# A long-convolution block: magnitudes summed before their products, two of five inverse tables used whole in f32, and a reordered start

## The chip, the cores and the metric

The kernel is one program on one core of a Trainium2 chip. The metric is the device time of one execution in microseconds (us); lower is better. Times stand as the median of a few runs. The profile is of one further execution.

## The reference, cut to what matters

The whole model is two blocks on 512 positions (528 with 16 meta positions), width 1024. The change touches the first layer alone, a gated long convolution over 2048 channels:

```
u = rmsnorm(h) @ w_in + b_in                       # 528 x 8192
x0, x1, v = split(short_conv(u[:, :6144])); z = u[:, 6144:]
h_fwd, h_bwd = filters(w1..w4) * decay / (sum |filters| + 1e-6)
taps = concat(h_fwd, 0, h_bwd[:0:-1])
y  = irfft(rfft(v * x1, 2T) * rfft(taps, 2T))[:T] + skip * (v * x1)
h += rmsnorm((y * x0 * silu(z)) @ w_out)
```

The transforms are products with cosine and sine tables. `sum |filters|` runs over positions and both directions and gives one number per channel. After this layer come a differential-attention layer and a second block (sparse attention and a mixture of experts); the change leaves both as they are.

## The kernel before, in words

TensorE does the work in one of two forms. A *split* operand is a pair of fp32r tiles, high part and low part; a product of two split operands is three fp32r products (high-high, high-low, low-high). A *whole* operand is a plain f32 tile, and its product is one call. A split costs ScalarE one cast (L328, or L282 for weights) and VectorE or GpSimd one subtraction (L329, or L263 for weights).

Python loops are unrolled. The framework orders each engine's instructions itself, by a simulated timeline; `issue_after(x)` queues the instructions of a block behind x on x's engine, and `high_priority` moves work forward. Every engine then runs its queue strictly in that order. A tile name has `bufs` slots; a new tile of the name waits until the slot's last reader is done.

**Start** (`small_vectors` L513, `load_x` L544). SP's queue loads x, then the small vectors `sva`, `svb`, `svc` (L516 to L526), then the weights `wraw` (L232). ScalarE squares and sums x in five pieces (L563), each into a slot of `hTd` (2 slots). x is transposed into PSUM tile `ps` (2 slots, L582), copied to `hTd` (L584), stored to DRAM (L588), scaled by gain and norm (`xnf`, L593) and split into `xh`, `xl`. The gains come from `vc`, the transposed `svc`. The first product of the layer needs `xh`, `xl`, a split weight, and a free slot of `ps`. The split of the first weight job is queued behind the scaling `normed` on VectorE, that of the second behind the copy `copied` (third pair of columns) on ScalarE.

**Spectra** (`filter_spectra` L701, interleaved with the first half of the input projection `hyena_in`, up to about 345 us). For each of 8 quarters q of 256 channels it forms even and odd filters for three tiles of positions (128, 128 and 9 rows), takes magnitudes `mg` on ScalarE (L741) and their maximum on VectorE (L745); GpSimd adds the two directions (L747). TensorE then sums over positions by products with a column of ones (L790): 2 halves of channels x 3 tiles of positions a quarter, whole f32, reduced on VectorE (L791). The spectra go to DRAM (`Hdram`).

**Convolution** (`hyena_conv` L852, about 545 to 720 us). The inverse tables `gm` come by GpSimd's queue (L864). For each of 8 quarters: `fold` makes even and odd parts, transposes and splits them; five frequency tiles m = 0 to 4 are formed by split products (`ph`, L188), multiplied by the spectrum `hsp` (loaded by ScalarE's queue, L954) on VectorE (L960 to L962) and combined on GpSimd into `o` (L964, L966). `o` is split for m < 4 into `oh`, `ol`; m = 4 (17 rows, kept in 64-row tiles `orem`, shown as `or`) is split by four 17-row instructions (L975, L976). `inverse` runs one quarter behind: for each of 2 channel tiles and 2 sides it accumulates 15 products into `ps` (3 for each m), and ScalarE, VectorE and GpSimd form y (L902 to L909), which is split at the end of the quarter. Behind the last quarter comes the output projection (`pj`, L811 to L815).

Of the kernel before, what the change touches and what calls it, by code (L numbers as in the profile page):

```python
# [10 lines left out]
FT = mybir.dt.float32  # L11
FR = mybir.dt.float32r
# [3 lines left out]
OP = mybir.AluOpType  # L16
# [26 lines left out]
def host_consts():  # L43
# [83 lines left out]
    G[4, 32:32 + 9, 1, :n] = ge_im[256:265]  # L127
    gh, gl = _hi_lo(G)
    c["idft"] = np.ascontiguousarray(np.stack([gh, gl], axis=2).transpose(0, 1, 2, 3, 4))

    inv = (F32(10000.0) ** (-np.arange(0, 64, 2, dtype=F32) / F32(64))).astype(F32)
# [194 lines left out]
def split(k, raw, hi, lo, lo_eng=None):  # L326
    nc = k.nc
    nc.scalar.copy(hi, raw)  # L328
    (lo_eng or nc.vector).tensor_tensor(lo, raw, hi.bitcast(FT), OP.subtract)  # L329

# [178 lines left out]
def small_vectors(k, A, pp):  # L509
# [4 lines left out]
    with tc.tile_pool(name="sv", bufs=1, reuse_waits="tile") as sp:  # L514
        a = sp.tile([128, 128], FT, name="sva")
        nc.sync.dma_start(a[0:64], A["hy_b_in"][0].rearrange("(r c) -> r c", c=128))  # L516
        nc.sync.dma_start(a[64:112], A["hy_conv_b"][0].rearrange("(r c) -> r c", c=128))
        nc.sync.dma_start(a[112:128], A["hy_skip"][0].rearrange("(r c) -> r c", c=128))
        b = sp.tile([128, 128], FT, name="svb")
        c = sp.tile([64, 128], FT, name="svc")  # L520
        cw = A["hy_conv_w"][0].rearrange("t (r c) -> (t r) c", c=128)
        nc.sync.dma_start(b, cw[0:128])
        nc.sync.dma_start(c[0:16], cw[128:144])
        for i, (n, l) in enumerate((("norm_pre", 0), ("norm_pre", 1), ("norm_post", 0), ("norm_post", 1),
                                    ("norm_mix_2", 0), ("norm_ffn_2", 0))):
            nc.sync.dma_start(c[16 + 8 * i:24 + 8 * i], A[n][l].rearrange("(r c) -> r c", c=128))  # L526
# [18 lines left out]
def load_x(k, A, sp, pp):  # L545
# [15 lines left out]
    for i, (t0, n) in enumerate(TT):  # L561
        scr = sp.tile([128, 2, T], FT, name="hTd", bufs=2).rearrange("p a b -> p (a b)")[:, 0:D]
        nc.scalar.activation(scr[:n], xt[:n, i], AF.Square, accum_out=ss[:n, i:i + 1])  # L563
    rs = sp.tile([128, 5], FT, name="rs")
# [13 lines left out]
    for d0 in range(0, KD, 2):  # L578
        p = pp.tile([128, 2, 512], FT, name="ps", bufs=2)
        for j in range(2):  # L580
            for i in range(4):
                nc.tensor.transpose(p[:, j, i * 128:(i + 1) * 128], xt[:, i, (d0 + j) * 128:(d0 + j + 1) * 128], k.ident)  # L582
        hT = sp.tile([128, 2, T], FT, name="hTd", bufs=2)
        copied = nc.scalar.copy(hT[:, :, 0:512], p)  # L584
# [6 lines left out]
        for j in range(2):  # L591
            xn = sp.tile([128, T], FT, name="xnf", bufs=2)
            normed = nc.vector.scalar_tensor_tensor(xn, hT[:, j], k.gain(0, d0 + j), rbs, op0=OP.mult, op1=OP.mult)  # L593
            split(k, xn, k.xh[:, d0 + j], k.xl[:, d0 + j], nc.gpsimd if j else None)
        if d0 == 0:
# [29 lines left out]
def first_projection(k, A, C, pp):  # L625

    nc, tc = k.nc, k.tc
    with ExitStack() as ctx:
# [17 lines left out]
        for i in range(3):  # L646
# [52 lines left out]
def filter_spectra(k, A, C, hs, sp, wk, pp):  # L699
# [11 lines left out]
    for q in range(E // Q):  # L711
# [10 lines left out]
        mag = {}  # L722
        msum = []
        for s, op in ((0, OP.add), (1, OP.subtract)):
# [7 lines left out]
            for kt, (t0, n) in enumerate(KT):  # L732
# [53 lines left out]
            nc.sync.dma_start(k.Hdram[q4, 9:17, 9 - s, co], hsr[0:8, 1])  # L786
        p = pp.tile([128, 512], FT, name="pab", bufs=2)[:, 0:8].rearrange("p (c k) -> p c k", c=2)
        for c in range(Q // 128):
            for kt, (t0, n) in enumerate(KT):
                nc.tensor.matmul(p[:, c, kt:kt + 1], msum[kt][:n, c * 128:(c + 1) * 128], k.ones[:n], start=True, stop=True)  # L790
        nc.vector.tensor_reduce(tot[:, 2 * q:2 * q + 2], p[:, :, 0:3], AX.X, OP.add)  # L791
    nc.vector.tensor_scalar(tot, tot, 1e-6, None, op0=OP.add)
# [60 lines left out]
def hyena_conv(k, A, C, pp):  # L853
# [3 lines left out]
    with ExitStack() as ctx:  # L857
# [3 lines left out]
        sp = ctx.enter_context(tc.tile_pool(name="hc", bufs=1, reuse_waits="tile"))  # L861
        gm = sp.tile([128, 5, 2, 2, 266], FR, name="gm")
# [10 lines left out]
        for i in range(2):  # L873
            for s in range(2):
                vrem[i, s] = k.fold.tile([128, Q], FR, name=f"vr{i}{s}", bufs=1)
                nc.vector.memset(vrem[i, s].bitcast(FT), 0.0)
                orem[i, s] = sp.tile([64, Q], FR, name=f"or{i}{s}")
                nc.vector.memset(orem[i, s].bitcast(FT), 0.0)
        his, los = [], []

        def inverse(q, oh, ol):
            yy = wk.tile([128, NC, T], FT, name="y", bufs=1)
            for c in range(NC):
# [4 lines left out]
                for s in range(2):  # L888
                    p = pi[:, s, 0:266]
                    parts = []  # L890
                    for m in range(5):
                        sel = (0 if m < 2 else 1) if s == 0 else (1 if m < 2 else 0)
                        if m == 4:
                            a, b, n = oh[m][:, fs], ol[m][:, fs], 64
                        else:
                            a, b, n = oh[m][:, sel, fs], ol[m][:, sel, fs], 128
                        g0, g1 = gm[0:n, m, 0, s], gm[0:n, m, 1, s]
                        parts += [(a, g0), (a, g1), (b, g0)]
                    mmacc(nc, p, parts)
# [42 lines left out]
        for q in range(NQ):  # L942
# [6 lines left out]
            for m in range(5):  # L949
# [12 lines left out]
                nc.vector.tensor_tensor(t2[:n, 1], p[:n, 1], hsp[:n, 0], OP.mult)  # L962
                o = fw.tile([128, 2, Q], FT, name="o")
                nc.gpsimd.tensor_tensor(o[:n, 0], t1[:n, 0], t1[:n, 1], OP.subtract)  # L964
                d = slice(32, 32 + n) if m == 4 else slice(0, n)
                nc.gpsimd.tensor_tensor(o[d, 1], t2[:n, 0], t2[:n, 1], OP.add)  # L966
                if m < 4:
                    oh[m] = wk.tile([128, 2, Q], FR, name=f"oh{m}")
                    ol[m] = wk.tile([128, 2, Q], FR, name=f"ol{m}")
                    split(k, o, oh[m], ol[m])  # L970
                else:
                    oh[m], ol[m] = orem[q % 2, 0], orem[q % 2, 1]
# [1303 lines left out]
```

## Time and profile before

| | |
|---|---|
| runs, median (lowest to highest) | 2360.93 us (2360.74 to 2366.43), 3 runs |
| profiled execution, its own time | 2362.28 us |
| its span | 2360.5 us |
| PE busy | 2219.6 us, 94% of the span, 14332 instructions |
| DVE (VectorE) busy | 1537.9 us, 65% |
| ACT (ScalarE) busy | 1070.5 us, 45% |
| POOL (GpSimd) busy | 706.2 us, 30% |
| DMA | 306.18 MB, mean 130 GB/s |

PE is TensorE's products, PEld its weight loads, SP the engine that only issues DMAs. Products are pipelined, so the busy time of PE says little where starts are close together: the distance from one start to the next is what a product costs. PEclk is the granted share of TensorE's clock, 1.00 for 2.4 GHz and 0.50 for 1.2 GHz. In square brackets stands how long an engine was idle before an instruction and what it waited for. Names are out<-in, numbers of slots left out; a row with xN merges N instructions in succession. Times of rows are us from the span's start.

### The profile page before, as it was taken

To read this page: it belongs to the slowest core of one execution; us is meant where nothing else is said; L and a number is where in the kernel's file an instruction comes from. 1 tells how busy PE (TensorE), PEld (TensorE's weight loads), DVE (VectorE), ACT (ScalarE), POOL (GpSimd) and SP (SyncE) were. 2 spreads that over 40 slices of the span, in tenths; PEclk is the share of its full clock that TensorE was granted. 3 is DMA by queue.
4 is the path that set the end of the run, shared out by engine and by line. 5 is a ranking of instruction groups with operands and counts; after the bars stand their busy time and mean duration, and the time that the engine had idled before them with its cause. 6 is when DMAs were issued, how large, how long until landed. Compare 5 with 4: busy or idle time off the path is not lost. (4 is left out here: it accounts for less than half of the span.)

```text
span 2360.5 us, 37091 instructions
## 1 busy us (share of the span) xinstructions
PE 2219.6 (94%) x14332; PEld 1832.0 (78%) x14332; DVE 1537.9 (65%) x2852; ACT 1070.5 (45%) x2173; POOL 706.2 (30%) x705
## 2 busy tenths in 40 slices
PE   7999999998999989999999998989999999799997
PEld 6899989998889988898888887977666666534443
DVE  7688774546985578777868854568768655434434
ACT  5566653432334456655656644534444443222221
POOL 4455451114651333332323324623111103100100
PEclk9999999999999989999999998989899999899999
DMA  6433332232217522111211124652221235599991
GB/s 224 131 100 117 95 101 90 90 90 92 57 52 222 155 82 72 54 41 50 72 54 54 58 69 144 176 151 55 67 81 59 72 107 211 186 368 424 421 370 74
DMA packets 242060, 306.18 MB, mean 130 GB/s; under 512 B 20648, under 2 KB 208436, under 8 KB 233306
## 3 DMA queue, kind: packets, MB, share of 16 engines
q1 hardware_dynamic: 203328, 245.90, 30.8%
q10 hardware_dynamic: 33002, 32.64, 4.6%
q0 software_dynamic: 5552, 25.25, 2.9%
q8 instruction: 113, 1.85, 0.3%
q14 instruction: 65, 0.53, 0.1%
HBM read 278.19 MB, written 25.58 MB: 129 GB/s over the span
## 5 line engine op out<-in xcount | busy, mean ns | idle before, releaser
L263 DVE TENSOR_TENSOR wlo<-wraw,whi 128x1024 fp32r<-128x1024 f32 (+2 forms) x201 | 225.6, 1135 | 150.6 <-ACT whi L282 142.6
L263 POOL TENSOR_TENSOR wlo<-wraw,whi 128x1024 fp32r<-128x1024 f32 (+1 forms) x91 | 181.2, 1999 | 475.0 <-ACT whi L282 345.5
L282 ACT CAST whi<-wraw 128x1024 fp32r<-128x1024 f32 x198 | 205.9, 1047 | 171.4 <-PE ps L813 50.3
L811 PE MATMUL ps<-xh,whi 128*128 128x264 f32 x1024 | 214.3, 286 | 5.4 <-ACT hTd L584 5.1
L813 PE MATMUL ps<-xl,whi 128*128 128x264 f32 x1024 | 214.0, 286 | 0.2 <-POOL xl L329 0.2
L815 PE MATMUL ps<-xh,wlo 128*128 128x264 f32 x1024 | 211.8, 285 | 0.0
L811 PE MATMUL pj<-xh,whi 128*128 128x512 f32 (+2 forms) x544 | 191.8, 355 | 4.9 <-DVE rr L1193 4.6
L813 PE MATMUL pj<-xl,whi 128*128 128x512 f32 (+2 forms) x544 | 189.7, 351 | 0.0
L815 PE MATMUL pj<-xh,wlo 128*128 128x512 f32 (+2 forms) x544 | 189.0, 350 | 0.4 <-DVE wlo L263 0.4
L811 PEld LDWEIGHTS ps<-xh,whi 128*128 128x128 f32 x1024 | 160.7, 189 | 7.5 <-ACT hTd L584 5.8
L813 PEld LDWEIGHTS ps<-xl,whi 128*128 128x128 f32 x1024 | 161.3, 189 | 2.0 <-issue 1.3
L815 PEld LDWEIGHTS ps<-xh,wlo 128*128 128x128 f32 x1024 | 160.8, 189 | 1.2 <-issue 0.8
L813 PE MATMUL pj<-vx,whi 128*128 128x256 f32 (+1 forms) x480 | 136.6, 286 | 0.7 <-DVE vx L329 0.7
L1302 ACT ACTIVATE p<-S,mx 128x528 f32<-128x528 f32 x128 | 89.8, 703 | 77.4 <-DVE mx L1300 42.6
L811 PEld LDWEIGHTS pj<-xh,whi 128*128 128x128 f32 x544 | 103.4, 191 | 19.5 <-DVE rr L1193 6.0
L815 PEld LDWEIGHTS pj<-xh,wlo 128*128 128x128 f32 x544 | 103.0, 191 | 13.1 <-DVE wlo L263 0.6
L813 PEld LDWEIGHTS pj<-xl,whi 128*128 128x128 f32 x544 | 103.2, 191 | 12.1
L1300 DVE TENSOR_REDUCE mx<-S 128x1 f32<-128x528 f32 x128 | 89.0, 700 | 13.7 <-PE S L1299 12.5
L2022 PE MATMUL gu<-wraw,Xs 128*64 128x512 f32 x400 | 97.3, 604 | 0.0
L813 PEld LDWEIGHTS pj<-vx,whi 128*128 128x128 f32 x480 | 91.5, 191 | 1.0 <-DVE vx L329 0.9
L1298 PE MATMUL S<-ks,qh 128*128 128x264 f32 x256 | 72.0, 302 | 11.9 <-ACT p L1302 11.7
L1656 ACT ACTIVATE P<-S,mx 128x128 f32<-128x128 f32 (+3 forms) x96 | 50.3, 530 | 70.1 <-PE pt L1673 55.3
(685 smaller groups left out, 6442.4 us busy)
## 6 DMA issues: line engine op xcount, KB each, us to landing
wraw<-in_w_gate_up_dram SPq DMA_DIRECT2D x50, 1024.0 KB
wraw<-in_hy_w_in_dram SPq DMA_DIRECT2D x32, 1024.0 KB
wraw<-in_da_w_in_dram SPq DMA_DIRECT2D x32, 1024.0 KB
wraw<-in_hy_w_out_dram SPq DMA_DIRECT2D x16, 1024.0 KB
wraw<-in_da_w_out_dram SPq DMA_DIRECT2D x16, 1024.0 KB
wraw<-in_w_down_dram SPq DMA_DIRECT2D x14, 1024.0 KB
wraw<-in_w_in_dram SPq DMA_DIRECT2D x20, 512.0 KB
whi<-in_w_down_dram SPq DMA_DIRECT2D x18, 512.0 KB
```

Of the source, the lines that this page charges most:

```text
L263: eng.tensor_tensor(l, r, h.bitcast(FT), OP.subtract)
L282: nc.scalar.copy(hf, vf)
L811: nc.tensor.matmul(ps[i], wh[:, kk, fsl], xh[:, kk, c], start=f, stop=False)
L813: nc.tensor.matmul(ps[i], wh[:, kk, fsl], xl[:, kk, c], start=False, stop=False)
L815: nc.tensor.matmul(ps[i], wl[:, kk, fsl], xh[:, kk, c], start=False, stop=l)
L1298: nc.tensor.matmul(S[:, i, 0:TH], qh[:, qs], ks[:, c], start=True, stop=False)
L1300: nc.vector.tensor_reduce(mx[:, m:m + 1], S[:, :, 0:TH], AX.XY, OP.max, negate=True)
L1302: nc.scalar.activation(p.rearrange("p (a b) -> p a b", a=2), S[:, :, 0:TH], AF.Exp, bias=mx[:, m:m + 1], accum_out=sm[:, m:m + 1])
L1656: nc.scalar.activation(p[:, m, 0:n], S[:, m, 0:n], AF.Exp, bias=mx[:, m:m + 1], accum_out=sm[:, m:m + 1])
L2022: mm = nc.tensor.matmul(ps[o], xs[:, kk, o], w[:, a], start=(kk == 0), stop=(kk == 7))
```

## The change

- Start: seven of the small loads (`svc`) move from SP's to GpSimd's queue. `hTd` has three slots. Two of the five squares of x run on VectorE. The first weight job's split is queued behind `normed` and also behind `copied`; the second's behind the cast `high` and the subtraction `low` of the first pair of columns.
- Spectra: GpSimd adds the magnitudes of the three tiles of positions into one tile; TensorE makes 2 products with ones a quarter, and VectorE copies the result.
- Convolution: the tables of m = 3 and m = 4 are kept whole in f32 (`gf`), half the bytes each; `o` of m = 3 and 4 is not split, and each is one whole f32 product instead of three fp32r ones.

```diff
+            c["idft2"] = G[3:5]                       # whole; idft (high, low) keeps G[0:3]
-        nc.sync.dma_start(c[0:16], cw[128:144])
+        nc.gpsimd.dma_start(c[0:16], cw[128:144])
-            nc.sync.dma_start(c[16 + 8 * i:24 + 8 * i], ...)
+            nc.gpsimd.dma_start(c[16 + 8 * i:24 + 8 * i], ...)
...
-        scr = sp.tile([128, 2, T], FT, name="hTd", bufs=2)...
-        nc.scalar.activation(scr[:n], xt[:n, i], AF.Square, accum_out=ss[:n, i:i + 1])
+        scr = sp.tile([128, 2, T], FT, name="hTd", bufs=3)...
+        if i in (1, 3):
+            nc.vector.scalar_tensor_tensor(scr[:n], xt[:n, i], 1.0, xt[:n, i], op0=OP.mult, op1=OP.mult,
+                                           accum_out=ss[:n, i:i + 1])
+        else:
+            nc.scalar.activation(scr[:n], xt[:n, i], AF.Square, accum_out=ss[:n, i:i + 1])
...
-        with tc.issue_after(k.paced["normed"]):
+        with tc.issue_after(k.paced["normed"]), tc.issue_after(k.paced["copied"]):
             k.W.split_to(1)
-        with tc.issue_after(k.paced["copied"]):
+        with tc.issue_after(k.paced["high"]), tc.issue_after(k.paced["low"]):
             k.W.split_to(2)
...
                     nc.gpsimd.tensor_tensor(mag[kt, 0][:n], mag[kt, 0][:n], mag[kt, 1][:n], OP.add)
-                    msum.append(mag[kt, 0])
+                    if kt:
+                        nc.gpsimd.tensor_tensor(mag[0, 0][:n], mag[0, 0][:n], mag[kt, 0][:n], OP.add)
...
-            for kt, (t0, n) in enumerate(KT):
-                nc.tensor.matmul(p[:, c, kt:kt + 1], msum[kt][:n, c * 128:(c + 1) * 128], k.ones[:n], ...)
-        nc.vector.tensor_reduce(tot[:, 2 * q:2 * q + 2], p[:, :, 0:3], AX.X, OP.add)
+            nc.tensor.matmul(p[:, c:c + 1], mag[0, 0][:, c * 128:(c + 1) * 128], k.ones, ...)
+        nc.vector.tensor_copy(tot[:, 2 * q:2 * q + 2], p[:, 0:2])
...
-        for m in range(5):
+        for m in range(3):
             nc.gpsimd.dma_start(gm[:, m], C["idft"][m])
+        for m in range(2):
+            nc.gpsimd.dma_start(gf[:, m], C["idft2"][m])
...
                         if m == 4:
-                            a, b, n = oh[m][:, fs], ol[m][:, fs], 64
+                            parts.append((oh[m][:, fs], gf[0:64, 1, s]))
+                        elif m == 3:
+                            parts.append((oh[m][:, sel, fs], gf[:, 0, s]))
...
-                    for s in range(2):
-                        d = slice(32 * s, 32 * s + 17)
-                        nc.scalar.copy(oh[m][d], o[d, s])
-                        nc.vector.tensor_tensor(ol[m][d], o[d, s], oh[m][d].bitcast(FT), OP.subtract)
+                nc.gpsimd.tensor_tensor(o[0], t1[:n, 0], t1[:n, 1], OP.subtract)
+                nc.gpsimd.tensor_tensor(o[1], t2[:n, 0], t2[:n, 1], OP.add)
+                if m < 3:
+                    split(k, whole, oh[m], ol[m])
```

## Rows read from the trace of the kernel before

**Rows 1.** Windows: stretch, length, PE, PEld, DVE, ACT, POOL busy, PEclk, DMA share, GB/s.

```profile
20.00:40.00 20.00, 13.66 (x90) 12.49 (x90) 19.93 (x30) 11.90 (x16) 13.12 (x13) 0.83 0.95 328
...
100.00:300.00 200.00, 195.52 (x1564) 182.47 (x1564) 152.94 (x273) 124.50 (x292) 101.92 (x98) 1.00 0.36 111
...
580.00:660.00 80.00, 77.36 (x587) 69.50 (x586) 76.66 (x145) 30.49 (x63) 51.02 (x54) 1.00 0.21 58
```

**Rows 2.** Timeline of the start: start us, us, engine line op out<-in xcount [idle<-releaser].

```profile
6.83 0.31 SPq L523 DMA_DIRECT2D svc<-in_hy_conv_w_dram  x1
...
12.17 60.71 SPq L232 DMA_DIRECT2D wraw<-in_hy_w_in_dram  x7
...
19.75 2.36 DVE L263 TENSOR_TENSOR wlo<-wraw,whi 128x1024 fp32r<-128x1024 f32 x2 [0.35 <-ACT whi L282]
...
22.49 1.34 DVE L329 TENSOR_TENSOR xl<-xnf,xh 128x528 fp32r<-128x528 f32 x1
23.06 1.01 ACT L584 COPY hTd<-ps 128x1024 f32<-128x1024 f32 x1 [1.32 <-DMA hdram<-hTd]
...
24.12 0.81 PE L811 MATMUL ps<-xh,whi 128*128 128x264 f32 x2 [4.38 <-ACT hTd L584]
```

**Rows 3.** Timeline around the products with ones of the first quarter.

```profile
99.75 0.28 PE L790 MATMUL pab<-ones,mg 128*128 128x1 f32 x2
...
99.89 0.49 PE L815 MATMUL ps<-xh,wlo 128*128 128x264 f32 x2
...
100.21 0.28 PE L188 MATMUL pab<-wabh,hs 128*128 128x256 f32 x1
```

**Rows 4.** Instructions of tile mg: duration min/median/max; then who waited (us, times).

```profile
L747 POOL TENSOR_TENSOR mg<-mg,mg x24: 712/880/2580, 93.0 to 340.7; 128x256 f32<-128x256 f32 x16, 9x256 f32<-9x256 f32 x8
...
  PE pab L790: 2.8, 4
```

**Rows 5.** Timeline: whole f32 products of 266 columns.

```profile
18.63 1.11 PE L685 MATMUL pab<-zf,w 33*64 33x266 f32 x4
```

**Rows 6.** Timeline: start of the convolution.

```profile
545.30 2.72 POOL L864 DMA_DIRECT2D gm<-const_idft_dram  x5 [0.30 <-POOL gt L838]
...
556.69 0.69 DVE L960 TENSOR_TENSOR t<-ph,hsp 128x512 f32<-128x512 f32 x1 [6.67 <-DMA hsp<-Hdram]
...
558.10 0.40 PE L188 MATMUL ph<-vh,dft 128*17 128x256 f32 x1 [5.20 <-DVE t L962]
```

**Rows 7.** Windows of PE alone: stretch, length, busy, PEclk, DMA share, GB/s.

```profile
558.00:559.00 1.00, 0.90 (x5) 0.50 0.00 0
...
609.89:629.34 19.45, 18.77 (x142) 1.00 0.21 57
```

**Rows 8.** Timeline inside one quarter of the convolution.

```profile
609.02 0.50 PE L188 MATMUL ph<-vr,dft 96*128 96x256 f32 x2 [0.53 <-DVE vr L938]
...
609.91 0.39 PE L188 MATMUL ps<-gm,or 64*128 64x266 f32 x1 [0.17 <-DVE or L976]
...
613.33 0.29 PE L188 MATMUL ps<-gm,ol 128*128 128x266 f32 x1
...
613.70 0.29 PE L188 MATMUL ps<-gm,ol 128*128 128x266 f32 x1
```

**Rows 9.** VectorE by line and shape, the quarter 609.89 to 629.34.

```profile
L329 DVE TENSOR_TENSOR ol<-o,oh 128x512 fp32r<-128x512 f32 x4 | 2.8, 696 | 0.0
```

**Rows 10.** Timeline: end of the convolution.

```profile
700.16 0.79 POOL L966 TENSOR_TENSOR o<-t 17x256 f32<-17x256 f32 x1
...
701.44 0.75 PE L188 MATMUL ps<-gm,or 64*128 64x266 f32 x4 [1.37 <-ACT or L975]
...
703.06 0.85 DVE L976 TENSOR_TENSOR or<-o,or 17x256 fp32r<-17x256 f32 x2
...
703.97 0.59 PE L188 MATMUL ps<-gm,or 64*128 64x266 f32 x1 [1.78 <-DVE or L976]
```

**Rows 11.** Window of all engines at that end.

```profile
700.00:710.00 10.00, 6.85 (x36) 5.87 (x36) 9.83 (x15) 5.24 (x8) 0.88 (x2) 0.83 0.01 4
```

More of the change, by code (lines that the diff above doesn't have):

```diff
@@ L327, in split @@
     nc = k.nc
-    nc.scalar.copy(hi, raw)
-    (lo_eng or nc.vector).tensor_tensor(lo, raw, hi.bitcast(FT), OP.subtract)
+    high = nc.scalar.copy(hi, raw)
+    low = (lo_eng or nc.vector).tensor_tensor(lo, raw, hi.bitcast(FT), OP.subtract)
+    return high.ins, low.ins
 def sin_reduced(k, pool, out, arg, n):
@@ L561, in load_x @@
     for i, (t0, n) in enumerate(TT):
-        scr = sp.tile([128, 2, T], FT, name="hTd", bufs=2).rearrange("p a b -> p (a b)")[:, 0:D]
-        nc.scalar.activation(scr[:n], xt[:n, i], AF.Square, accum_out=ss[:n, i:i + 1])
+        scr = sp.tile([128, 2, T], FT, name="hTd", bufs=3).rearrange("p a b -> p (a b)")[:, 0:D]
+        if i in (1, 3):
[3 more added lines that the diff above has]
+            nc.scalar.activation(scr[:n], xt[:n, i], AF.Square, accum_out=ss[:n, i:i + 1])
     rs = sp.tile([128, 5], FT, name="rs")
@@ L582, in load_x @@
                 nc.tensor.transpose(p[:, j, i * 128:(i + 1) * 128], xt[:, i, (d0 + j) * 128:(d0 + j + 1) * 128], k.ident)
-        hT = sp.tile([128, 2, T], FT, name="hTd", bufs=2)
+        hT = sp.tile([128, 2, T], FT, name="hTd", bufs=3)
         copied = nc.scalar.copy(hT[:, :, 0:512], p)
@@ L593, in load_x @@
             normed = nc.vector.scalar_tensor_tensor(xn, hT[:, j], k.gain(0, d0 + j), rbs, op0=OP.mult, op1=OP.mult)
-            split(k, xn, k.xh[:, d0 + j], k.xl[:, d0 + j], nc.gpsimd if j else None)
+            high, low = split(k, xn, k.xh[:, d0 + j], k.xl[:, d0 + j], nc.gpsimd if j else None)
+            if d0 == 0:
+                k.paced["high" if j else "low"] = high if j else low
         if d0 == 0:
@@ L786, in filter_spectra @@
             nc.sync.dma_start(k.Hdram[q4, 9:17, 9 - s, co], hsr[0:8, 1])
-        p = pp.tile([128, 512], FT, name="pab", bufs=2)[:, 0:8].rearrange("p (c k) -> p c k", c=2)
+        p = pp.tile([128, 512], FT, name="pab", bufs=2)
         for c in range(Q // 128):
-            for kt, (t0, n) in enumerate(KT):
-                nc.tensor.matmul(p[:, c, kt:kt + 1], msum[kt][:n, c * 128:(c + 1) * 128], k.ones[:n], start=True, stop=True)
-        nc.vector.tensor_reduce(tot[:, 2 * q:2 * q + 2], p[:, :, 0:3], AX.X, OP.add)
+            nc.tensor.matmul(p[:, c:c + 1], mag[0, 0][:, c * 128:(c + 1) * 128], k.ones, start=True, stop=True)
+        nc.vector.tensor_copy(tot[:, 2 * q:2 * q + 2], p[:, 0:2])
     nc.vector.tensor_scalar(tot, tot, 1e-6, None, op0=OP.add)
@@ L861, in hyena_conv @@
         sp = ctx.enter_context(tc.tile_pool(name="hc", bufs=1, reuse_waits="tile"))
-        gm = sp.tile([128, 5, 2, 2, 266], FR, name="gm")
-        for m in range(5):
+        gm = sp.tile([128, 3, 2, 2, 266], FR, name="gm")
+        gf = sp.tile([128, 2, 2, 266], FT, name="gf")
+        for m in range(3):
             nc.gpsimd.dma_start(gm[:, m], C["idft"][m])
+        for m in range(2):
+            nc.gpsimd.dma_start(gf[:, m], C["idft2"][m])
         O = {}
@@ L876, in hyena_conv @@
                 nc.vector.memset(vrem[i, s].bitcast(FT), 0.0)
-                orem[i, s] = sp.tile([64, Q], FR, name=f"or{i}{s}")
-                nc.vector.memset(orem[i, s].bitcast(FT), 0.0)
+            orem[i] = sp.tile([64, Q], FT, name=f"or{i}")
+            nc.vector.memset(orem[i], 0.0)
         his, los = [], []
@@ L893, in inverse @@
                         if m == 4:
-                            a, b, n = oh[m][:, fs], ol[m][:, fs], 64
-                        else:
-                            a, b, n = oh[m][:, sel, fs], ol[m][:, sel, fs], 128
-                        g0, g1 = gm[0:n, m, 0, s], gm[0:n, m, 1, s]
-                        parts += [(a, g0), (a, g1), (b, g0)]
+                            parts.append((oh[m][:, fs], gf[0:64, 1, s]))
+                        elif m == 3:
+                            parts.append((oh[m][:, sel, fs], gf[:, 0, s]))
+                        else:
+                            a, b = oh[m][:, sel, fs], ol[m][:, sel, fs]
+                            g0, g1 = gm[:, m, 0, s], gm[:, m, 1, s]
+                            parts += [(a, g0), (a, g1), (b, g0)]
                     mmacc(nc, p, parts)
@@ L962, in hyena_conv @@
                 nc.vector.tensor_tensor(t2[:n, 1], p[:n, 1], hsp[:n, 0], OP.mult)
[L963 to L970, printed above, removed]
-                else:
-                    oh[m], ol[m] = orem[q % 2, 0], orem[q % 2, 1]
-                    for s in range(2):
-                        d = slice(32 * s, 32 * s + 17)
-                        nc.scalar.copy(oh[m][d], o[d, s])
-                        nc.vector.tensor_tensor(ol[m][d], o[d, s], oh[m][d].bitcast(FT), OP.subtract)
+                if m == 4:
+                    o = oh[m] = orem[q % 2]
+                    o = (o[0:n], o[32:32 + n])
+                else:
+                    o = fw.tile([128, 2, Q], FT, name="o") if m < 3 else wk.tile([128, 2, Q], FT, name="o3")
+                    if m == 3:
+                        oh[m] = o
+                    else:
+                        oh[m] = wk.tile([128, 2, Q], FR, name=f"oh{m}")
+                        ol[m] = wk.tile([128, 2, Q], FR, name=f"ol{m}")
+                        whole = o
+                    o = (o[:, 0], o[:, 1])
+                nc.gpsimd.tensor_tensor(o[0], t1[:n, 0], t1[:n, 1], OP.subtract)
+                nc.gpsimd.tensor_tensor(o[1], t2[:n, 0], t2[:n, 1], OP.add)
+                if m < 3:
+                    split(k, whole, oh[m], ol[m])
             pend.append((q, oh, ol))
```

6 lines of the change are left out of this document (3 added, 3 removed).

## The prediction, made before the result was known

> **What bounds the kernel now.** I read the windows by stage first, because the chain of waits does not reach back into the changed layer. Three kinds of stretch appear [rows 1]. From 100 to 300 us PE is busy 195.5 of 200 us and VectorE 153: TensorE's queue is the bound, and a product less is time less. From 20 to 40 us VectorE is busy 19.93 of 20 and PE 13.7 at a mean clock of 0.83: the ramp hangs on VectorE. From 580 to 660 us PE shows 77.4 and VectorE 76.7 of 80: both are near the bound. So I read starts and waits there from the timeline. The edges of the convolution are different again: PE stands idle for 5.20 us at its start [rows 6] and 1.37 and 1.78 us at its end [rows 10].
>
> **The change, part by part** (against the profiled execution, 2362.28 us, a span of 2360.5 and 1.8 around it; the median of the runs is 1.35 us below it).
>
> *Start.* PE waits 4.38 us and begins the layer's products at 24.12, released by the third copy to `hTd` at 23.06, which itself waited 1.32 us for the store of the first `hTd` [rows 2]. The third slot removes that wait. Next late is VectorE: the low part of the first weight runs from 19.75 to 22.11, the low part of x from 22.49 to 23.83 [rows 2]. The products of two high parts need neither and can start before, those with the weight's low part at 22.1, and only the third kind waits for 23.8: I take 2 us of the 4.38. The fourth `hTd` will still wait for the same store, but it holds only the second `ps` slot, needed later. The seven loads leave SP's queue, where they lie between 6.83 and the first weight load at 12.17 [rows 2]: that load is issued some 5.3 us earlier, and all later SP loads behind it. On GpSimd they come ahead of the inverse root of the norm; At the 0.31 us of SP's one [rows 2] they take GpSimd 2 us, and 5.3 if they take as long there as SP's whole stretch. That is hidden while the sums of squares are not done; without that cover the gains `vc` and with them every `xnf` slip by as much. The two squares on VectorE cost about 1.2 us each (half of the 2.36 us for two 1024-column instructions [rows 2]) at a time when it has only memsets behind it; ScalarE is freed of as much. First split behind `copied`: with the slot free that copy no longer comes at 23.06, so the wait costs nothing; if the copy stayed there, `whi`, `wlo` and the first product would come some 5 us later than now. Behind that waiting cast on ScalarE stand the casts `xh`, for which VectorE, GpSimd and PE wait. Second split behind `high` and `low`: earlier than now, nothing on the path. As VectorE is full until 40 us, the ramp gives back part of any larger gain. **I take -2.0; bounds -4.4 (the whole wait) and +5.**
>
> The Trainium skill ("SBUF — State Buffer", section "SBUF: two separate sides") warns that loads issued by GpSimd are held up while VectorE runs an operation that holds the port they share. By that rule the seven moved loads could land up to 2.4 us later, the length of the two squares, and this term would be about 0. No row here shows such a load beside such an operation.
>
> *Spectra.* With ones, TensorE has 6 products a quarter before and 2 after, so 32 fewer in 8 quarters. Each is two instructions. Two of them and the two ordinary products behind them take 99.75 to 100.21, 0.46 us [rows 3]; an ordinary one takes 0.123 (613.33 to 613.70 holds three [rows 8]), so one product with ones costs 0.46 - 0.25 = 0.21 us: 32 x 0.21 = 6.7 us off the bound engine. Added are two GpSimd additions a quarter, of 0.88 us in the middle and 2.58 at most, and they stand in one chain ahead of the product; today PE waits 2.8 us in all, four times, for such sums [rows 4]. Behind a waiting product stand the input projection's products, and the next quarter's first magnitude on ScalarE, as it rewrites the tile. I take 2 us more waiting over the 8 quarters, since the order lets other products go ahead. VectorE's copy for its reduction: no difference. **-4.7; bounds -9.5 (6.7 and all the 2.8) and +7.4 (both additions exposed every quarter, 8 x 1.76 - 6.7).**
>
> *Convolution, its first wait.* PE waits 5.20 us from the chain hsp, L960 to L962, ph; hsp's load landed at 556.69, 11.4 us after the loads of the tables began at 545.30 [rows 6], which fill the DMA engines. The tables shrink from five of equal size to three and two halves, by 20%: 0.2 x 11.4 = 2.3 us. Behind the wait PE runs at 0.50 of its clock [rows 7]; a shorter idle may spare some of it, for which I add 0.7. Memsets and five issues stay as hidden as they are. **-3.0; bounds -5.2 and 0** (hsp late for another reason).
>
> *Convolution, a quarter.* Removed: 4 groups x 6 = 24 fp32r products of 0.123 us, 2.95 us. Added: 8 whole products. A whole f32 product of 266 columns is two instructions (L685 has four for two products) that start (1.11 - 0.385) / 3 = 0.242 us apart, where 0.385 is the length of the last [rows 5]; 16 x 0.242 = 3.87 us. PE gains 0.92 us of work. The quarter lasts 19.45 us [rows 7], of which 0.53 and 0.17 are waits for VectorE's splits [rows 8], so PE needs 18.75 now and 19.67 after. VectorE loses one 0.7 us subtraction [rows 9] and the pair of 0.85 [rows 10], so its 18.64 becomes about 17.1 and those waits should go. So a quarter is 0.2 us longer, PE-bound. A change between whole and split weights is not in it; where rows 3 show one, the second ordinary product starts late within the 0.46. Four groups at 0.1 each would be 0.4. ScalarE's three casts less lie beside 70% idle; GpSimd's work stays, and its results now go straight to PE. **7 quarters: +1.5; bounds -5 (the waits go and the added work fits under them) and +9.**
>
> The Trainium skill ("Perfetto Trace Analysis", section "Engine Utilization") puts TensorE's rate for FP32_LOW_HIGH at one half. By that a whole product would be one pass at 0.242 us, a quarter's work would fall by 1.0 instead of rising by 0.9, and the kernel come out near 2336. L685's four instructions for two products speak against it.
>
> *Convolution, its end.* The last quarter's inverse has nothing to hide behind. PE waits for the casts and the subtractions of `or`, the last at 703.06 and 0.85 long, and goes on at 703.97; the data themselves were ready on GpSimd at 700.95 [rows 10]. Without the split PE goes on about 701.0: with 0.5 us of work done between, 2.5 us. Its clock is 0.83 over these 10 us [rows 11], 1.7 us of work lost, which should go with the idle. Against it 0.7 us for the dearer products. Next late are y and its split on VectorE, full with 9.83 of 10 us [rows 11], but part of that is work for the next layer that can be passed. **-3.5; bounds -5.2 and +1.**
>
> Sum: -2.0 - 4.7 - 3.0 + 1.5 - 3.5 = -11.7 us; 2362.28 - 11.7 = 2350.6, and 1.35 lower as a median: **2349**.
>
> **Rivals.** (a) *The edges are refilled.* Behind the start and the end of the convolution VectorE is the full engine [rows 1, 11]; if it sets the time there, the start, first-wait and end terms give 2 us together instead of 8.5, and the sum is -5.2: 2356. For it: 9.83 of 10. Against: the waits named end on a load and on `or`, not on other work.
> (b) *Slower: the ones wait for GpSimd.* One place, the head of PE's queue at the end of each quarter of the spectra. It decides when the added wait passes (11.7 + 2.0 + 7) / 8 = 2.6 us a quarter, the length of one slow addition [rows 4]; both additions at twice their usual length would be 3.5 us: 28 - 2 - 11.7 = +14, 2375. For it: PE is in order, and the addition varies from 0.71 to 2.58 us. Against: the present three sums cost 2.8 us in all.
> (c) *Whole products cost half of what I take*, one start of 0.242 us instead of two. PE then needs 18.75 - 2.95 + 1.94 = 17.7 us a quarter and VectorE 17.1: 7 x -1.7 instead of +1.5, 2336. For it: VectorE has the room. Against: the count of L685.
> (d) *Whole products cost more:* with 0.4 us a quarter for changes of form, and with the 0.7 of waits remaining, +1.3 a quarter instead of 0.2: 2357. For it: the late second product in rows 3. Against: VectorE has lost the work that made PE wait.
>
> **How the numbers follow.** Forecast 0.52 (its own range 2343 to 2354), (a) 0.18, (b) 0.10, (c) 0.05, (d) 0.15. 0.3% is about what a measurement of this kernel can tell from no change, 7 us: below 2354 is faster, above 2368 slower. Faster: 0.48 of the forecast, 0.05 of (c), 0.12 of (a) and (d): 0.65. Slower: 0.09 of (b). The rest is 0.26. The range leaves out (c) and most of (b): 2338 to 2361.
>
> **What will show it.** First product before 23 us and no wait on `hdram`. L790 with a third of its instructions, and PE's waits for `mg` near 5 us. hsp's wait near 4.4 us at the start of the convolution. A quarter at 19.4 to 19.9 us with VectorE below 18. No wait of PE on VectorE at the end, and a full clock there. A quarter above 20.5, or waits of PE on GpSimd's sums above 10 us, would make me wrong; a quarter below 18.5 would mean that my price for the whole products is.

## The result, and the profile after

The changed kernel is **slower**: 2382.69 us (median of 6 runs, 2377.13 to 2387.72) against 2366.35 of the kernel before beside it (6 runs); the ratio is 1.0074, 95% interval 1.0059 to 1.0089. I had said 2349, and slower with a chance of 0.09. The profiled execution of the kernel after, 2387.72 us (span 2385.9), is the longest of its six, that of before one of the shortest of its own, so the traces differ by 25.4 us and the medians by 16.3.

The windows of the stretches of [rows 1, 11], after:

```profile
20.00:40.00 20.00, 13.94 (x79) 12.47 (x78) 19.90 (x29) 10.41 (x14) 12.09 (x11) 0.74 0.84 290
100.00:300.00 200.00, 191.32 (x1542) 179.11 (x1542) 153.59 (x266) 122.10 (x282) 103.68 (x104) 1.00 0.36 111
580.00:660.00 80.00, 74.09 (x482) 61.47 (x481) 61.23 (x117) 22.79 (x43) 49.02 (x47) 0.94 0.17 48
700.00:710.00 10.00, 7.10 (x36) 4.93 (x34) 9.96 (x18) 4.56 (x6) 7.87 (x8) 0.81 0.11 30
```

In the convolution (580 to 660) no engine is as full as before: VectorE fell from 76.66 to 61.23 of 80 us, PE from 77.36 to 74.09, with 482 instructions for 587, at a clock of 0.94. So PE waits. PE's waits over the whole convolution, before and then after (us in total, times, longest):

```profile
PE ph L188 <- DVE t L962: 6.8, 2, 5.2
PE ps L188 <- DVE or L976: 2.3, 4, 1.8
PE ps L188 <- ACT or L975: 1.9, 2, 1.4
PE ph L188 <- DVE vr L938: 1.6, 3, 0.5
PE ps L188 <- DVE ol L329: 0.9, 2, 0.4
```

```profile
PE ph L189 <- DVE t L975: 8.7, 7, 2.8
PE ps L189 <- POOL or L989: 5.6, 3, 2.2
PE ps L189 <- DVE ol L330: 4.3, 3, 2.9
PE pab L948 <- DVE vl L330: 0.4, 2, 0.2
```

One of the three waits on `or`, in the timeline of after:

```profile
612.97 0.68 DVE L973 TENSOR_TENSOR t<-ph,hsp 17x512 f32<-17x512 f32 x1 [0.47 <-DMA hsp<-Hdram]
...
613.75 2.31 POOL L988 TENSOR_TENSOR or<-t 17x256 f32<-17x256 f32 x1
...
614.24 1.24 DVE L330 TENSOR_TENSOR vx<-y,gt 128x1056 fp32r<-128x1056 f32 x1
615.41 1.27 DVE L330 TENSOR_TENSOR vl<-pab,vh 128x512 fp32r<-128x512 f32 x2
616.14 0.72 POOL L989 TENSOR_TENSOR or<-t 17x256 f32<-17x256 f32 x1
616.91 0.49 PE L189 MATMUL ps<-gf,or 64*128 64x266 f32 x1 [1.67 <-POOL or L989]
```

A sum of 17 rows takes GpSimd 0.72 us, but 2.31 beside VectorE's subtraction of two tiles, and PE's queue stands until both sums are done; for 3.4 us from 617.5 the clock is at half. These sums were no faster in the kernel before (0.73 to 2.84 us). There PE stood behind the casts and subtractions that followed them, for 4.2 us in all (L975 and L976 in the first list).

Each trace in stages (us, from starts of products). The convolution runs from the last product of the input projection to the first of the output projection (`pj<-gt`), attention from the last `S<-xh` or `S<-xl` (near 850 us) to the first `pj<-yh` (near 1435). "Half" is the time within attention at which the granted clock is at half; the last column is the 95% interval of the ratio to before:

| kernel | projection ends | convolution | attention | half | ratio |
|---|---|---|---|---|---|
| before | 542.5 | 167.8 | 584.2 | 31.2 | |
| after | 535.1 | 181.8 | 594.5 | 52.7 | 1.0059-1.0089 |
| e1_no_conv | 535.0 | 170.1 | 590.4 | 37.6 | 0.9971-1.0014 |
| e2_conv_only | 540.2 | 178.7 | 587.1 | 34.3 | 1.0037-1.0072 |
| e3_start_only | 547.2 | 171.3 | 587.0 | 27.4 | 1.0036-1.0078 |
| e4_spectra_only | 531.1 | 169.5 | 587.0 | 34.4 | 0.9937-0.9973 |
| e5_ready_tiles | 541.1 | 171.2 | 585.6 | 30.8 | 1.0278-1.0328 |
| e6_dve_sums | 542.3 | 183.2 | 579.9 | 20.6 | 1.0043-1.0090 |
| e7_loads_only | 550.8 | 172.6 | 594.5 | 48.7 | 1.0044-1.0093 |
| e8_spectra_rest | 542.8 | 166.4 | 589.8 | 40.8 | 1.0009-1.0044 |
| e9_loads_rs_first | 549.2 | 167.9 | 582.8 | 24.5 | 1.0012-1.0046 |
| e10_spectra_start_rs_first | 532.9 | 171.4 | 583.3 | 27.6 | 0.9948-0.9979 |
| e11_whole3_only | 539.7 | 168.7 | 586.1 | 30.7 | 0.9995-1.0023 |
| e12_whole4_only | 542.0 | 181.7 | 587.1 | 34.1 | 1.0022-1.0062 |
| e13_all_but_start | 530.9 | 176.7 | 587.1 | 34.1 | 1.0002-1.0039 |
| e14_spectra_conv_first | 532.9 | 169.3 | 586.6 | 34.3 | 0.9968-1.0000 |
| e15_start_unpaced | 540.0 | 169.8 | 592.7 | 51.7 | 0.9976-1.0020 |
| e16_after_rs_first | 534.7 | 181.1 | 582.7 | 23.9 | 1.0010-1.0050 |
| e17_both_orders | 537.2 | 167.7 | 592.9 | 51.7 | 0.9995-1.0022 |

How far one trace can be trusted: six kernels with the same code ahead of the convolution (before, e2, e5, e6, e11, e12) end the projection at 539.7 to 542.5.

So after against before, in the traces: projection -7.4, convolution +14.0, attention (unchanged code) +10.3, the rest of the layers +8.5. In that rest, too, the clock is lower: from attention's end to the kernel's end it is at half for 101.2 us, against 82.6 before.

### The profile page after: what moved, and what is told of

Its sections match the earlier page's. It is cut to its first block, busy times and chain, and to the rows that moved or that the text cites. A ratio compares the mean times of both kernels' runs of the same rounds, so it can differ in the third digit from the quotient of the medians.

```text
span 2385.9 us, 36772 instructions
## 1 busy us (share of the span) xinstructions
PE 2238.8 (94%) x14204; PEld 1837.9 (77%) x14204; DVE 1542.0 (65%) x2830; ACT 1059.8 (44%) x2145; POOL 723.2 (30%) x728
## 5 line engine op out<-in xcount | busy, mean ns | idle before, releaser
L264 DVE TENSOR_TENSOR wlo<-wraw,whi 128x1024 fp32r<-128x1024 f32 (+2 forms) x201 | 230.5, 1158 | 153.6 <-ACT whi L283 143.2
L189 PE MATMUL ph<-fh,dft 128*128 128x256 f32 (+2 forms) x384 | 80.6, 281 | 5.4 <-ACT hsr L790 4.2
L1313 PE MATMUL S<-ks,qh 128*128 128x264 f32 x256 | 73.5, 308 | 12.9 <-ACT p L1317 12.8
```

Source lines behind the costliest of these rows:

```text
L189: nc.tensor.matmul(out, l, r, start=(i == 0), stop=(i == n - 1))
L264: eng.tensor_tensor(l, r, h.bitcast(FT), OP.subtract)
L1313: nc.tensor.matmul(S[:, i, 0:TH], qh[:, qs], ks[:, c], start=True, stop=False)
```

## Experiments

### Each part alone

e1: the convolution and its tables as before; e2, e3, e4: the kernel before with the convolution, the start, or the spectra changed. Their edits are those hunks of the diff.

> The changed kernel with the convolution and its tables as before; the start and the spectra stay changed. Theory (the convolution part loses, the two others gain): the last product of the first projection starts near 535 as in the changed kernel, the convolution lasts about 167 us as before (an hour's worth less than the 181.6 of the changed kernel does not matter here: 167 against 181.6 decides), and the time is about 7 us under the kernel before: ratio 0.997. Rival A (the unchanged attention code loses because the order of its instructions was recomputed after any change): convolution 167, but the stretch from the first product on gt to the last po is again some 10 us longer, and the ratio is 1.000 to 1.002. Rival B (the convolution lost because everything ahead of it came earlier): the convolution still lasts about 180, ratio 1.003.

> The kernel before with the convolution part alone: m = 3 and m = 4 whole, smaller tables. Theory: start and projection as before (last product near 542.5), the convolution lasts about 180 us instead of 167.7, and the time is 13 to 20 us over the kernel before: ratio 1.006 to 1.008. Rival A (attention's order): the convolution 180 us and a further 8 to 10 us in attention: ratio near 1.010. Rival B: the convolution lasts about 168, ratio 1.000.

> The kernel before with the start alone changed (loads on GpSimd, squares on VectorE, third slot, splits queued behind the copies). Theory (the term of the prediction): first product near 20.7, the products on xl no earlier than 24.7, -2 us by the end of the projection: ratio 0.999. Rival: nothing is left of it at the end of the projection, since VectorE fills the ramp until 40 us: ratio 1.000. Rival A (attention's order): 5 to 10 us longer behind the convolution: ratio 1.003.

> The kernel before with the spectra alone changed (magnitudes added on GpSimd, 32 products with ones less). Theory (the term of the prediction): the projection ends 4.7 us earlier, near 537.8; ratio 0.998. Rival: PE gets back the whole 6.7 us and the two sums cost it nothing: ends near 535.8. Rival A (attention's order): 5 to 10 us longer behind the convolution: ratio 1.001 to 1.003.

Measured: the convolution part costs 10.9 us in its stage. The other two don't both gain: the spectra gain 11.4 us by the end of the projection (8.6 to 11.4 against the six kernels above), and the start **loses** 4.6 alone and 3.9 beside the spectra. The -7.4 that seemed to bear out both terms is a larger gain less a loss. Rival B falls: the convolution is near its old length in e1 (170.1) and long in e2 (178.7). Rival A is not settled here: attention is 6.2 us longer than before in e1 and 2.8 in e2 and e3, and the ratio of e1, 0.9993, lies between both forecasts. Spectra alone is faster than both kernels: 2357.05 us, 0.9955.

The medians of the runs say more than the stages. Against before, the convolution alone costs 12.9 us, the start alone 13.0, and the spectra alone gain 10.2. That is +15.7 together, against +16.3 for the whole change. So the start costs as much as the convolution, though only 4.6 us of it stand at the end of the projection; the rest falls into code that it does not touch.

### The convolution: waits, price, or place

e5 has the convolution part alone, but its whole products, those of m = 3 likewise, read a constant tile. Its output is then another, and what follows attention takes 72.7 us longer than before, so only its convolution is compared:

```diff
-parts.append((oh[m][:, fs], gf[0:64, 1, s]))
+parts.append((ready[0:64, 0, fs], gf[0:64, 1, s]))
```

> The kernel before with the convolution part alone (as e2_conv_only, whose convolution lasts 178.6 us against 167.7), but the whole products of m = 3 and m = 4 read a tile that was filled once at the start; GpSimd's sums still run, and nothing in the inverse waits for those of m = 3 and 4. Its output is not the reference's. Theory (the new waits are the cost: in e2 PE stands 6.1 us for GpSimd's sums of m = 4, and 3 us more at half clock): the waits on or are gone, the convolution is 168 to 171 us, the time within 4 us of the kernel before (ratio 1.000 to 1.002). Rival (the whole products are the cost: 16 instructions of 0.224 us and changes of form at 0.32, for 24 of 0.124): the convolution stays at 176 to 179 us, ratio 1.004 to 1.005. Rival (the order in which the other waits fall, VectorE's t ahead of ph): the convolution is 174 to 176.

171.2 us against 178.7 of e2: of the 10.9 that the part costs, 7.5 hang on those tiles becoming ready, 3.4 remain as dearer work and other order. e6 instead moves m = 4's sums:

```diff
-nc.gpsimd.tensor_tensor(o[0], t1[:n, 0], t1[:n, 1], OP.subtract)
-nc.gpsimd.tensor_tensor(o[1], t2[:n, 0], t2[:n, 1], OP.add)
+eng = nc.vector if m == 4 else nc.gpsimd
+eng.tensor_tensor(o[0], t1[:n, 0], t1[:n, 1], OP.subtract)
+eng.tensor_tensor(o[1], t2[:n, 0], t2[:n, 1], OP.add)
```

> As e2_conv_only, with the two 17-row sums of m = 4 on VectorE instead of GpSimd. Theory (GpSimd's slow sums at the head of PE's queue cost 6.1 us of idle PE and the clock behind it): the three waits of some 2 us on or are gone, the convolution is 170 to 174 us, ratio 1.001 to 1.003. Rival (price of the whole products): 177 to 180 us, as e2. Rival (VectorE near its bound): its added 14 sums of 0.3 to 0.4 us make PE wait for VectorE instead, and the convolution is 180 to 184 us.

The waits on `or` are gone, but PE waits 9.1 us for VectorE's `vl` in six places, and the stage takes 183.2: the third theory.

```profile
PE ph L189 <- DVE vl L330: 9.1, 6, 2.1
```

e11 and e12 are the kernel before with one group whole:

> The kernel before with m = 3 whole and m = 4 split as before. Theory (the waits on GpSimd's sums of m = 4 and the order around them are the main cost, dearer work the smaller): the convolution lasts 167 to 172 us (before 167.8, e2 178.7). Rival (price of the whole products and changes of form): 173 us or more, more than half of e2's loss, as m = 3 has half of the whole products.

> The kernel before with m = 4 whole and m = 3 split as before. Theory (GpSimd's sums of m = 4 stand at the head of PE's queue): three or more waits of some 2 us on or, the convolution lasts 174 to 178 us. Rival (price): 171 to 173 us, half of e2's loss, without the waits on or.

m = 3 whole costs 0.9 us, m = 4 whole 13.9, more than foreseen and more than both together in e2. Nor are its waits on `or` three of some 2 us: two are 0.23 us, and one at the end is 7.18. PE's waits on `or` in e12, and the last one in its timeline:

```profile
PE ps L189 <- POOL or L978: 7.6, 3, 7.2
```

```profile
704.28 8.23 POOL L978 TENSOR_TENSOR or<-t 17x256 f32<-17x256 f32 x1
...
706.98 2.34 DVE L264 TENSOR_TENSOR wlo<-wraw,whi 128x1024 fp32r<-128x1024 f32 x2
...
709.58 2.34 DVE L264 TENSOR_TENSOR wlo<-wraw,whi 128x1024 fp32r<-128x1024 f32 x2
...
712.56 0.81 PE L189 MATMUL ps<-gf,or 64*128 64x266 f32 x1 [7.18 <-POOL or L978]
```

The sum that takes 0.72 us takes 8.23 while VectorE splits the output projection's weights, and ends 0.6 us behind the last of them; the clock is at half for 23.9 us from 704.9. The Trainium skill ("SBUF — State Buffer", section "SBUF: two separate sides") says that a VectorE operation with two inputs in SBUF and a GpSimd operation that reads SBUF share a port pair, and that the one that comes second is fully blocked; these rows agree.

e14 keeps both groups whole and changes only their place; e13 is its control, the changed kernel with the start as before.

```diff
-for m in range(5):
+for m in (3, 4, 0, 1, 2):
```

> The changed kernel with the start as before: spectra and convolution changed. In attention's order 81 of some 3470 products of TensorE stand elsewhere than in the kernel before, in the changed kernel 1208. Theory (each part costs what it costs alone, and attention's loss follows its order): the projection ends at 531 as in e4, the convolution lasts 178 to 181 us, the stretch of attention 583 to 588 us (584.2 before, 594.5 in the changed kernel), and the time is 10 to 15 us under the changed kernel: ratio 1.000 to 1.002. Rival (attention loses because its data come at another time or the clock falls, whatever its order): attention 592 to 596, ratio 1.004 or above.

> As e13_all_but_start, with the order of the groups changed in the convolution's loop and in the products: 3, 4, 0, 1, 2 instead of 0 to 4, so that GpSimd's sums for the whole ones are done long before PE's queue reaches them. Theory (what costs is that the sums of m = 4 come last and stand directly ahead of PE): no wait on or above 0.5 us, the convolution 168 to 173 us. Rival (whichever group comes last makes PE wait, now m = 2 with its cast and its subtraction): 176 to 180 us. Rival (price): 178 or more with no such wait.

PE's waits on `or` in e13, and all of its waits in e14:

```profile
PE ps L189 <- POOL or L982: 5.5, 3, 2.2
```

```profile
PE ph L189 <- DVE t L968: 4.9, 2, 3.9
PE ph L189 <- DVE vl L330: 2.6, 1, 2.6
PE ps L189 <- DVE ol L330: 1.4, 2, 1.0
PE ps L189 <- ACT oh L329: 0.7, 1, 0.7
```

176.7 against 169.3 us, with the clock at half for 10.2 us of either: place decides. (For e13 178 to 181 were foreseen; its projection and its attention came as foreseen.) In e14 no wait on `or` is left, and m = 2, now last with its split, makes PE wait 1.4 us for `ol` and 0.7 for `oh`. In their new place the sums also take 0.74 us at most, but for one of 1.19. With the waits gone the convolution is about as long as with the split products (e4 169.5, before 167.8), so whole products bring nothing either; by the runs e14 (0.9984) is even a little behind e4 (0.9955).

### The start

e7 moves the seven loads alone; e8 is the spectra with the rest of the start; e9, e10 and e16 (e7, e1 and the changed kernel) put `rs` first:

```diff
+with tc.issue_after(turned.ins) if d0 >= 4 else ExitStack():   # turned: the transposes of rs
     nc.tensor.transpose(p[:, j, i * 128:(i + 1) * 128], xt[:, i, ...], k.ident)
```

> The kernel before with one edit of the start alone: the seven loads of svc on GpSimd. Theory (with the inverse root behind them, the transposes of rs stand behind eight more transposes of xt and that of svc in PE's queue, rbs comes 3 to 4 us late, and VectorE, full from 20 to 40 us, never gets it back): rs is transposed near 18.2 instead of 14.3, VectorE idles 3 us before it, the projection ends 3 us later than in the kernel before, near 545.5, and the unchanged attention code loses as in e1 and e3. Rival (another edit of the start, the splits queued behind the copies or the squares on VectorE, is what costs): rs near 15, the projection ends at 542 or earlier.

> The spectra part with the rest of the start (third slot, two squares on VectorE, splits queued behind the copies), the seven loads left on SP. Theory: rs is transposed near 14.5 to 15, the first projection ends earlier than in e4_spectra_only (531.1 for its last product), near 529, and the time is 1 to 3 us under e4: ratio 0.994 to 0.995. Rival (another edit of the start costs): the projection ends near 534, ratio 0.997 or above.

> As e7_loads_only (seven loads of svc on GpSimd, nothing else; projection ended at 550.8), with one more edit: the transposes of xt for the third and fourth hTd are queued behind the transposes of rs. Theory (e7 loses because rs stands behind those transposes, rbs comes late, and VectorE idles 3 us before a stretch in which it is full): rs at 14.5 to 15.5, projection ends at 539 to 543 (the kernel before 542.5). Rival (the loads cost by something else, the clock or the order of VectorE's work after the start): rs early, and the projection still ends at 547 or later.

> As e1_no_conv (spectra and start changed, convolution as before; projection ended at 535.0, rs at 17.3), with the transposes of rs queued ahead of those for the third and fourth hTd. Theory: rs at 14.5 to 15.5, projection ends at 528 to 531 (e4_spectra_only without the start 531.1), ratio 0.994 to 0.997, the rest being attention's order. Rival (the start's cost is not rs): the projection ends at 534 to 536 as in e1, ratio 0.999.

The loads alone cost 8.3 us by the end of the projection, where 3 were foreseen. My theory was the order of PE's queue, visible in after:

```profile
12.21 1.56 POOL L573 TENSOR_TENSOR rs<-ss,mhalf 16x1 f32<-16x1 f32 x2 [0.51 <-DVE ss L572]
...
14.33 3.12 PE L588 MATMUL ps<-ident,xt 128*128 128x128 f32 x16
17.38 0.27 PE L531 MATMUL ph<-ident,svc 64*128 64x64 f32 x1
17.58 0.81 PE L579 MATMUL pab<-ident,rs 128*128 128x128 f32 x5
18.27 0.77 DVE L582 COPY rbs<-pab 128x512 f32<-128x512 f32 x2 [0.36 <-PE pab L579]
```

`rs` is ready near 13.8, but 16 transposes of `xt` stand ahead (14.28 before), so VectorE, full until 40 us, starts the normalisation late. It is half of the answer. Of the products with the weight's low part the 33rd (42.8 us before) is 4.3 us late in e7 and 0.1 in e9. But in e10, with the rest of the start, it is again 3.2 us behind e4, as e1 was (3.3). VectorE's time from 14 us to that product shows what changed: e4 has 26.2 us of work and 2.7 idle, e1 27.0 and 5.8, e10 28.6 and 3.3. With `rs` first most of the idle time is gone, but the sines of the filters (`arg`, `sinred`) take 14.5 us ahead of that product, against 10.7 in e1. And e9 loses another 6.5 us between 70 and 290 us, where its clock is at half twice (72.3 and 147.4, 3.4 us each) and no one wait explains it. e8, which missed both of its forecasts (542.8), shows that the rest leans on the loads: with them on SP, the weights come late, and PE stands 7.0 us for `hTd`, copied behind them. e15 takes away the new places of the weights' splits:

```diff
-with tc.issue_after(k.paced["normed"]), tc.issue_after(k.paced["copied"]):
+with tc.issue_after(k.paced["normed"]):
     k.W.split_to(1)
-with tc.issue_after(k.paced["high"]), tc.issue_after(k.paced["low"]):
+with tc.issue_after(k.paced["copied"]):
     k.W.split_to(2)
```

> As e10_spectra_start_rs_first (projection ended at 532.9), with the splits of the first weights queued behind the normalisation and the copy as in the kernel before, so that VectorE does x's low part ahead of the weights' low parts. Theory (that order costs the ramp its 3 us, VectorE being full from 20 to 40 us): the first products at 20 to 21 us and by 43 us at least 2 us ahead of e10; the projection ends at 527 to 530, ratio 0.993 to 0.995. Rival (nothing of an earlier start is left, as VectorE has the same work to do until 40 us): the ramp's end and the projection's as in e4 or later, 531 to 534, ratio 0.995 to 0.997.

A miss: 1.2 us of the 3.2 come back at that product, but the projection ends 7.1 us later than in e10, which is not explained either. At the end of the projection no form of the start beats leaving it alone.

In the medians of the runs `rs` first gives back more than there: 11.3 us (e7 to e9), 6.3 (e1 to e10) and 7.1 (the changed kernel to e16), each kernel against before beside it, where the projection's end gives 1.6, 2.1 and 0.4. In the traces the difference lies mostly in attention, which the next section takes up.

### The unchanged attention, and both orders repaired

> The changed kernel with one edit: the transposes of xt for the third and fourth hTd queued behind those of rs. In attention's order 651 products stand elsewhere than in the kernel before instead of 1208, as in e5, e6 and e9, whose attention lasted 580 to 586 us. Theory (attention's loss follows its order): attention 580 to 587 us instead of 594.5, the convolution near 181, the projection's end at 532 to 535, ratio 1.001 to 1.003. Rival (the loss is not the order's): attention 592 to 596, ratio 1.006 or above.

Attention fell to 582.7 us, as the order theory said. But e15 refutes that theory: in e10 and e15 all of attention's some 3,530 products stand in the order of the kernel before, and it lasts 583.3 and 592.7. What goes with its length is the clock: 27.6 and 51.7 us at half. After against before it is 52.7 against 31.2, and half of the difference, 10.7, is about the loss, 10.3 us (between e10 and e15 half would be 12.1, and 9.4 were lost). The windows of attention, before and after, with PEclk third from the end:

```profile
850.60:1434.80 584.20, 545.34 (x3535) 487.87 (x3533) 431.31 (x837) 339.87 (x708) 192.15 (x223) 0.97 0.19 58
```

```profile
857.40:1451.90 594.50, 553.95 (x3532) 496.67 (x3530) 436.25 (x838) 340.19 (x708) 191.39 (x223) 0.96 0.19 57
```

Attention less half of its time at half clock is 568.6 us before, 568.1 after, and 566.9 to 573.3 in all 19 traces: it varies by 6.4 us, attention itself by 14.6. The clock also differs between runs of one kernel: the span times what the mean granted clock lacks of 1 is 68 to 100 us in 130 runs of the kernel before (medians of 83 to 88 in five sets) and 86 to 100 in the six of after (median 93). What makes it fall more often stays open; e15 and e17 have `rs` first and the low clock all the same.

> The changed kernel with two edits of order: the groups of the convolution's loop and of its products in the order 3, 4, 0, 1, 2 (as in e14), and the transposes of xt for the third and fourth hTd behind those of rs (as in e16). Theory (each loss sits where the single experiments put it): the projection ends at 532 to 535, the convolution lasts 168 to 172 us instead of 181.8, no wait of PE on or above 0.5 us, and the time is 2354 to 2363 us, ratio 0.996 to 0.999. Rival (the parts disturb each other, so that what one repairs another loses): the convolution is 174 us or more, or the ratio is above 1.000.

The convolution lasts 167.7 us instead of 181.8, with no wait on `or` among PE's: that repair holds inside the whole change. But the projection ends at 537.2, attention has 51.7 us at half clock, and the ratio is 1.0008: no gain is left. By its bounds the rival holds; which part disturbs which is not shown.

## Why the prediction was wrong, by its own steps

**The convolution, a quarter: the step that failed** ("VectorE loses one 0.7 us subtraction and the pair of 0.85 ... and those waits should go. So a quarter is 0.2 us longer, PE-bound", and "its results now go straight to PE"). VectorE did lose the work, and the two waits that I named are gone. But from the second `s` of a quarter (L902 before, L915 after) to that of the next the seven quarters took 20.61, 21.28, 21.60, 26.61, 20.27, 22.78 and 19.79 us, 152.9 in all against 133.6 before: +19.4 where I took +1.5 and bounded at +9 (the end of the last inverse, a term of its own below, is in the seventh). My own sign of being wrong, a quarter above 20.5 us, came true. I priced the split that left and not what it had hidden: GpSimd's sums of the last group, now directly ahead of an in-order PE (e5, e11, e12, e14). Such a wait can cost clock too: behind the one at 616.91 it is at half for 3.4 us. Over the whole convolution PE's waits rose from 13.5 to 19.0 us and the time at half clock from 10.2 to 17.1. Taking half of that, some 5 us of the +14.0 are left for the dearer products, an estimate; eight quarters at my +0.92 would be 7.4. My rival (b) had this mechanism, PE behind GpSimd's sums, at another place. A slip without effect: ScalarE was idle for 62% there ([rows 1]), not 70%.

**The price of a whole product** was near: two instructions 0.224 us apart (I took 0.242) inside a tile, and the change between whole and 64-row tiles, which I left out, 0.32. Rival (c) is dead: in after 626.18 to 627.36, four instructions of two products of m = 3 and 4 take 1.18 us.

```profile
626.18 0.61 PE L189 MATMUL ps<-gf,o 128*128 128x266 f32 x2
626.72 0.71 PE L189 MATMUL ps<-gf,or 64*128 64x266 f32 x2
627.36 0.66 PE L944 MATMUL pab<-ident,ed 128*128 128x128 f32 x4
```

(The row with `gf,o` is one product of m = 3, that with `gf,or` one of m = 4.) By this the half rate of the Trainium skill ("Perfetto Trace Analysis", section "Engine Utilization") does not give one product per 0.24 us here.

**Its first wait**: right, -2.4 for -3.0. [rows 6] had 5.20 us, after has 2.79:

```profile
547.72 0.29 PE L189 MATMUL ph<-vh,dft 128*17 128x256 f32 x1 [2.79 <-DVE t L975]
```

The clock beside it was spared too: the 6.8 us at half from 557.1 in the kernel before have no counterpart in after, where the clock of the convolution first falls at 617.5. From the projection's end to the first of the `s` above after takes 29.0 us for 36.7.

**Its end**: -3.5 foreseen, a loss measured: the last of the seven quarters took 19.79 us for 18.06 before. The waits on `or` of [rows 10] are gone, but next late was VectorE, full with 9.96 of 10 us, the risk of rival (a): PE waits 2.90 us for `ol`, and the clock there is 0.81 instead of 0.83 [rows 11].

```profile
706.63 0.59 PE L189 MATMUL ps<-gm,ol 128*128 128x266 f32 x1 [2.90 <-DVE ol L330]
```

**Spectra**: the sign right, the size about twice mine: -8.6 to -11.4 for -4.7, around my bound of -9.5. Two terms were mis-sized. I read the price of a product with ones, 0.21 us, from [rows 3], where one product (two instructions) stands between others. Most stand in blocks; here four products of the kernel before hold PE from 106.45 to 107.60, 0.29 each:

```profile
106.45 1.22 PE L790 MATMUL pab<-ones,mg 9*128 9x1 f32 x8
107.60 0.39 PE L813 MATMUL ps<-xl,whi 128*128 128x264 f32 x1
```

All 48 took 12.4 us from start to next start, 0.26 each. And PE's waits for the sums, which I raised by 2 us, fell from 2.8 [rows 4] to 1.4 in e4.

**Start, the second step that failed**: the sign wrong. By the projection's end it is +3.9 to +4.6 for -2.0, inside the bounds; by the medians of the runs +13.0 alone and +8.1 beside the spectra (e1 against e4), beyond the bound of +5. The first product came at 20.67, no wait on `hdram`, as said. I named the hazard (the gains "and with them every `xnf` slip") but took it as covered by the sums of squares; with the loads alone what slipped was `rs` in PE's queue, and I had not asked what the added loads do to the order in which the planner puts PE's work. That is not all: with `rs` back in place VectorE's other work stands in the way (e10). What the start costs behind the projection stays open. What the Trainium skill says of loads issued by GpSimd ("SBUF — State Buffer", section "SBUF: two separate sides") was not tested: the last of the seven went out at 4.98, and VectorE's first square began at 6.62.

**Attention and the rest** had no term. The +10.3 us goes with the clock, and so, by the same measure (half of 18.6 us more at half clock), may the +8.5. Part of both, like 9 of the 25.4 us, belongs to this execution and not to the change: the medians differ by 16.3.

## What to carry to other kernels

A step taken out of a chain takes its cover along: before unsplitting an operand, ask which instruction then stands directly ahead of the in-order engine, and on which engine. Put such a producer early in the loop, not last: the order of five groups decided 7 to 13 us here. Try the parts of a change one by one, and by the whole time as well as by their stages: of three, one alone made this kernel faster, and a sum of two right-looking stages hid a loss.

## What the runs showed of the hardware

GpSimd's 17-row addition takes 0.72 us, or 2.31, or 8.23, by what VectorE subtracts beside it. Unchanged attention lasted 579.9 to 594.5 us over these traces, with 20.6 to 52.7 us at half clock: the shortest has the least, the two longest 48.7 and 52.7. A whole f32 product of 266 columns is two instructions, 0.224 us from start to start; two products of different shape took 1.18 us (after, 626.18).
